# Expert 1's input in sixteen short transfers, and the input of experts 2 and 3 in four

## The chip, the cores and the metric

The kernel runs on one core of a Trainium2 chip. The core has a matrix engine (TensorE, PE in the profile), three engines for elementwise work (VectorE is DVE, ScalarE is ACT, GpSimd is POOL), and SyncE (SP), which here only issues transfers. Transfers between the chip's main memory (DRAM) and the on-chip memory of 128 partitions are carried by 16 DMA engines, which all queues share: a transfer is issued by SyncE, ScalarE or GpSimd and is cut into packets, and the packets are spread over DMA engines. The metric is the device time of one execution in microseconds (us); lower is better.

## The reference

Eight experts, each a two-layer network with its own weights and biases, on 256 rows of 512 numbers:

```python
n_experts, capacity, hidden, expert_hidden = 8, 256, 512, 2048
h = np.matmul(x, w1) + b1[:, np.newaxis, :]
h = np.maximum(h, 0)
return (np.matmul(h, w2) + b2[:, np.newaxis, :]).astype(np.float32)
```

All inputs and the output are float32 in DRAM. Each expert's w1 and w2 are 4 MB each in DRAM.

## The kernel before, in words

Weights are converted to fp16 by the transfer itself, which only GpSimd's queue does here, so each w1 and each w2 is a transfer of 2 MB as written on the chip (128 partitions of 16,384 bytes). w1 and w2 have a pool of three buffers each. Two experts in the list HALVED (6 and 7) load their w2 in two halves, so that their second product can begin on the first.

x reaches the chip in two ways. x of experts 0 and 1 (`nXF32 = 2`, lines 187 to 190) is loaded as float32 by SyncE, 128 rows of 4,096 bytes each (row p of the tile holds rows 2p and 2p + 1 of x); VectorE then casts it to fp16 (line 201). x of experts 2 and 3 is one transfer of GpSimd's queue that converts to fp16 on the way, and x of experts 4 to 7 another (`load_x`, lines 72 to 80; `X_LOADS` gives the first expert and their number). In these, a tile row holds rows of one expert only, and the tile's 128 partitions are shared by the experts. VectorE transposes each x in 32 x 32 blocks (`transposes`, lines 95 to 112) into xT, a pool of two buffers, with the next expert's transposes placed in the middle of an expert's first product (line 135).

`first_product` (lines 114 to 136) makes, for each of sixteen column blocks j, four matmuls into one PSUM tile, which ScalarE then turns into hT with bias and relu (line 128). The bias is read from b1T, which VectorE makes by four transposes of `b1_rows` (line 208). `second_product` (lines 166 to 185) runs three experts later (`LAG = 3`): one small matmul puts b2 into PSUM (line 171), and 2 x 16 matmuls add hT times w2 (line 178). `store` (lines 142 to 164) copies the two PSUM tiles to an output tile, one half by VectorE and one by ScalarE. Experts 0 to 3 and 4 to 5 share an output tile each, which GpSimd's queue writes out at the end (`flush`, lines 138 to 140). Expert 6 is stored in three transfers (`PARTS`, line 40): rows 0 to 24 by SyncE, 25 to 120 by ScalarE, 121 to 127 by SyncE. Expert 7 is one transfer of SyncE.

The order of the work is partly written out and partly chosen by the scheduler of the Tile framework. GpSimd's transfers and all matmuls are kept in program order (`ordered`): w1 of expert 0, the biases b2 and b1, and then what the list `ring` (lines 215 to 225) gives for each step of the main loop: x where `X_LOADS` names the step, w1 of the next experts, w2 of earlier ones. VectorE's order is the scheduler's. In the program before it is: cast x0, sixteen transposes of x0, cast x1, seven transposes of x1, four of the bias, nine of x1, and then the other experts'. The framework gives the transfers of SyncE and ScalarE together eight completion semaphores, and those of GpSimd eight others, in turn; a transfer that takes a semaphore again waits for the one that had it before.

Of the kernel before, what the change touches and what calls it, by code (L numbers as in the profile page):

```python
# [10 lines left out]
def kernel(  # L11
# [9 lines left out]
    nc = tc.nc  # L21
# [4 lines left out]
    P = 128  # L26
    nTB = T // P
# [11 lines left out]

    PARTS = {E - 2: ((0, 25, False), (25, 121, True), (121, 128, False))}  # L40
    nXF32 = 2
    X_LOADS = {2: 2, 4: 4}

    def ordered(ins):
        return tc.keep_in_program_order(ins)
# [26 lines left out]
    def load_x(first, n):  # L72

        R = n * T // P
        t = x_pool.tile([P, R, H], fp16, tag=f"x{first}", name=f"x{first}")
        ordered(nc.gpsimd.dma_start(  # L76
            out=t, in_=x[first : first + n].rearrange("e (p r) h -> (e p) r h", r=R)
        ))
        for i in range(n):
            x16[first + i] = (t, i * (P // n), R)  # L80

    def load_w1(e):
        w1_sb[e] = w1_pool.tile([P, nKC, M], fp16, tag="w1", name="w1sb")
        ordered(nc.gpsimd.dma_start(  # L84
            out=w1_sb[e], in_=w1[e].rearrange("(p kc) m -> p kc m", kc=nKC)
        ))
# [100 lines left out]
    x32 = []  # L187
    for e in range(nXF32):
        x32.append(out_pool.tile([P, nTB, H], fp32, tag="out", name="x32"))
        nc.sync.dma_start(out=x32[e], in_=x[e].rearrange("(p tb) h -> p tb h", tb=nTB))  # L190
    load_w1(0)
    ordered(nc.gpsimd.dma_start(  # L192
        out=b2_sb,
        in_=b2.rearrange("e h -> (e h)").rearrange("(o f) -> o f", o=1),
# [4 lines left out]
    for e in range(nXF32):  # L199
        t = x_pool.tile([P, nTB, H], fp16, tag=f"x{e}", name=f"x{e}")  # L200
# [6 lines left out]
    for b in range(nB):  # L207
        nc.vector.transpose(  # L208
            out=b1T[b * B : (b + 1) * B, nB - 1 - b : nB - 1 - b + nJ * B],
            in_=b1_rows.rearrange("r (i j) -> r j i", j=nJ),  # L210
# [5 lines left out]
    for s in range(1, E + LAG - 1):  # L216
        if s < E:
            if s in X_LOADS:
                ring.append((s - 2, load_x, (s, X_LOADS[s])))
            ring.append((s - 2, load_w1, (s,)))  # L220
        if s >= LAG:
            ring.append((s - 2, load_w2, (s - LAG,)))
# [43 lines left out]
```

## Time and profile before

| | us |
|---|---|
| median of 2 runs (181.54 to 181.85) | 181.69 |
| span of the profiled execution, from the first to the last instruction | 179.8 |
| TensorE matmul busy | 129.0 (72%) |
| VectorE busy | 87.8 (49%) |
| ScalarE busy | 70.2 (39%) |
| GpSimd busy | 13.4 (7%) |

The profile is of one execution; no whole time of that execution is shown beside its span, so the span stands against the median of the runs. Main memory was read 71.39 MB and written 4.19 MB, 420 GB/s over the span. The chain that ended last is put down by 55% to DMA and by 32% to TensorE. Times in rows are from the span's start. A row of a timeline has start, length, engine, line, operation, tiles and count, and in brackets the idle time before it and what ended it; "q" behind an engine's name marks its own sequencer, where transfers are issued. A row of DMA issues has tiles, issuer, count, KB of one and the median from issue to landing.

### The profile page before, as it was taken

To read this page: it belongs to the slowest core of one execution; us is meant where nothing else is said; L and a number is where in the kernel's file an instruction comes from. 1 tells how busy PE (TensorE), PEld (TensorE's weight loads), DVE (VectorE), ACT (ScalarE), POOL (GpSimd) and SP (SyncE) were. 2 spreads that over 40 slices of the span, in tenths; PEclk is the share of its full clock that TensorE was granted. 3 is DMA by queue.
4 is the path that set the end of the run, shared out by engine and by line. 5 is a ranking of instruction groups with operands and counts; after the bars stand their busy time and mean duration, and the time that the engine had idled before them with its cause. 6 is when DMAs were issued, how large, how long until landed. Compare 5 with 4: busy or idle time off the path is not lost.

```text
span 179.8 us, 1957 instructions
## 1 busy us (share of the span) xinstructions
PE 129.0 (72%) x784; PEld 86.2 (48%) x784; DVE 87.8 (49%) x125; ACT 70.2 (39%) x151; POOL 13.4 (7%) x28
## 2 busy tenths in 40 slices
PE   0005199959995930999869597969788887999740
PEld 0004089948993410794369244943387433343310
DVE  1999933985000199999999998000600020301010
ACT  0000569947993050482189005940298020111010
POOL 7000003020201010001000001000100020020000
PEclk9999999987999995599999799996999999999995
DMA  5999999999999999999999999999999999999995
GB/s 215 252 230 195 233 208 201 233 228 200 215 231 193 219 230 222 197 226 230 208 204 230 219 200 226 230 211 200 230 219 201 226 211 208 217 211 221 324 456 215
DMA packets 3828, 40.56 MB, mean 226 GB/s; under 512 B 460, under 2 KB 476, under 8 KB 1132
## 3 DMA queue, kind: packets, MB, share of 16 engines
q0 software_dynamic: 3232, 38.35, 96.5%
q1 hardware_dynamic: 476, 1.70, 2.4%
q10 hardware_dynamic: 112, 0.39, 0.5%
q8 instruction: 6, 0.10, 0.2%
q14 instruction: 2, 0.02, 0.0%
HBM read 71.39 MB, written 4.19 MB: 420 GB/s over the span
## 4 chain that ended last, share of the span: by engine, by line
DMA 55%; PE 32%; ACT 3%; another core or an unknown queue 3%; POOL 2%; issue 1%; POOLq 0%; ACTq 0%
DMA w1sb<-in_w_dram 43%; PE po L178 16%; PE ph L121 15%; DMA w2sb<-in_w_dram 12%; ACT out L157 3%; PE po L171 1%; POOL w1sb L84 1%; ACT hT L128 1%; POOL w2sb L93 0%; POOL x L76 0%; POOL b_sb L192 0%; POOL b_rows L196 0%; POOLq L250 0%; ACTq L128 0%
## 5 line engine op out<-in xcount | busy, mean ns | idle before, releaser
L121 PE MATMUL ph<-xT,w1sb 128*128 128x256 f16 x512 | 64.9, 293 | 34.1 <-DMA w1sb<-in_w_dram 21.5
L121 PEld LDWEIGHTS <-w1sb 128*128 128x128 f16 x512 | 59.8, 147 | 40.1 <-DMA w1sb<-in_w_dram 31.8
L178 PE MATMUL po<-w2sb,hT 128*128 128x512 f16 x256 | 60.0, 394 | 9.8 <-DMA w2sb<-in_w_dram 9.8
L112 DVE STREAM_TRANSPOSE xT<-x 32x256 f16<-32x256 f16 (+1 forms) x64 | 53.0, 888 | 26.0 <-DMA x<-in_x_dram 19.2
L128 ACT ACTIVATE hT<-ph,b1T 128x256 f16<-128x256 f32 x128 | 56.2, 474 | 14.4 <-PE ph L121 14.2
L178 PEld LDWEIGHTS <-hT 128*128 128x128 f16 x256 | 25.5, 101 | 44.1 <-issue 17.8
L156 DVE COPY out<-po 32x512 f32<-32x512 f32 (+2 forms) x22 | 15.1, 688 | 53.7 <-PE po L178 53.5
L157 ACT COPY out<-po 32x512 f32<-32x512 f32 (+2 forms) x22 | 12.7, 579 | 68.8 <-PE po L178 68.6
L109 DVE STREAM_TRANSPOSE xT<-x 32x256 f16<-32x256 f16 x32 | 14.0, 436 | 0.5
L93 POOL DMA_DIRECT2D w2sb<-in_w_dram x10 | 5.3, 534 | 71.6 <-PE po L178 71.6
L84 POOL DMA_DIRECT2D w1sb<-in_w_dram x8 | 4.8, 601 | 64.1 <-PE ph L121 63.3
L128 ACT ACT_TABLE_LOAD x1 | 1.3, 1283 | 20.1 <-DVE b1T L208 20.1
L171 PE MATMUL po<-b_sb,ones 1*128 1x512 f16 x16 | 4.8, 379 | 0.0
L208 DVE STREAM_TRANSPOSE b1T<-b_rows 32x512 f32<-32x512 f32 x4 | 4.1, 1031 | 0.1
L201 DVE CAST x<-x 128x1024 f16<-128x1024 f32 x2 | 1.4, 694 | 3.1 <-DMA x<-in_x_dram 3.1
L171 PEld LDWEIGHTS <-ones 1*128 1x128 f16 x16 | 0.9, 92 | 2.1 <-issue 2.1
L140 POOL DMA_DIRECT2D out_dram<-out x2 | 1.1, 538 | 9.8 <-ACT out L157 9.8
L76 POOL DMA_DIRECT2D x<-in_x_dram x2 | 1.1, 552 | 0.0
L197 DVE MEMSET ones<- 1x128 f16 x1 | 0.2, 165 | 0.8 <-PEq L250 0.8
L196 POOL DMA_DIRECT2D b_rows<-in_b_dram x1 | 0.5, 515 | 0.0
L192 POOL DMA_DIRECT2D b_sb<-in_b_dram x1 | 0.5, 513 | 0.0
L250 POOL MEMSET const-float32-0.0<- 128x1 f32 x1 | 0.1, 99 | 0.2 <-issue 0.2
(3 smaller groups left out, 0.3 us busy)
## 6 DMA issues: line engine op xcount, KB each, us to landing
w1sb<-in_w_dram POOLq DMA_DIRECT2D x8, 2048.0 KB, 34.8
w2sb<-in_w_dram POOLq DMA_DIRECT2D x6, 2048.0 KB, 47.2
w2sb<-in_w_dram POOLq DMA_DIRECT2D x4, 1024.0 KB, 23.2
out_dram<-out POOLq DMA_DIRECT2D x1, 2048.0 KB, 19.0
x<-in_x_dram SPq DMA_DIRECT2D x2, 512.0 KB, 3.7
x<-in_x_dram POOLq DMA_DIRECT2D x1, 1024.0 KB, 31.2
out_dram<-out POOLq DMA_DIRECT2D x1, 1024.0 KB, 14.9
x<-in_x_dram POOLq DMA_DIRECT2D x1, 512.0 KB, 24.0
```

The lines of the kernel that those rows point to most:

```text
L84: ordered(nc.gpsimd.dma_start(out=w1_sb[e], in_=w1[e].rearrange("(p kc) m -> p kc m", kc=nKC)))
L93: ordered(nc.gpsimd.dma_start(out=w2_sb[e][:, lo : lo + half], in_=src[:, lo : lo + half]))
L109: nc.vector.transpose(out=out[:, :, g, :, 0, :], in_=block[:, :, :, 0, :])
L112: nc.vector.transpose(out=out[:, tb, g], in_=block[:, tb])
L121: ordered(nc.tensor.matmul(out=ph, lhsT=w1_sb[e][:, kc, :].rearrange("p (q j) -> p q j", j=nJ)[:, :, j], rhs=xT[e][:, kc, :], start=(kc == 0),
L128: nc.scalar.activation(out=hT[e][:, j, :].rearrange("p (tb k i) -> p tb k i", tb=nTB, k=split), in_=ph.rearrange("p (tb i k) -> p tb k i", ...
L156: nc.vector.tensor_copy(out=out_sb[at : at + rows, k * nTB, :], in_=po[0][part])
L157: nc.scalar.copy(out=out_sb[at : at + rows, k * nTB + 1, :], in_=po[1][part])
L171: ordered(nc.tensor.matmul(out=t, lhsT=ones1, rhs=b2_sb[0:1, e * H : (e + 1) * H], start=True, stop=False,))
L178: ordered(nc.tensor.matmul(out=po[tb], lhsT=hT[e][:, j, tb * P : (tb + 1) * P], rhs=w2_sb[e][:, j, :], start=False, stop=(j == nJ - 1),))
L201: nc.vector.tensor_copy(out=t, in_=x32[e])
L208: nc.vector.transpose(out=b1T[b * B : (b + 1) * B, nB - 1 - b : nB - 1 - b + nJ * B], in_=b1_rows.rearrange("r (i j) -> r j i", j=nJ),)
```

## The change

The load of x1 is cut into sixteen transfers of 15, 14, 13, ..., 2, 1 and 8 rows, issued by SyncE and ScalarE in turn; together they are the same 128 rows. The load of x of experts 2 and 3 is cut into four transfers of 112, 7, 6 and 3 rows, all by GpSimd, in the place of the one before. The load of x of experts 4 to 7 stays whole.

```diff
+    RUNS = ((15, False), (14, True), (13, False), (12, True), (11, False), (10, True), (9, False),
+            (8, True), (7, False), (6, True), (5, False), (4, True), (3, False), (2, True),
+            (1, False), (8, True))
+    X_PARTS = (112, 7, 6, 3)
...
-        ordered(nc.gpsimd.dma_start(
-            out=t, in_=x[first : first + n].rearrange("e (p r) h -> (e p) r h", r=R)
-        ))
+        src = x[first : first + n].rearrange("e (p r) h -> (e p) r h", r=R)
+        at = 0
+        for rows in X_PARTS if first == 2 else (P,):
+            ordered(nc.gpsimd.dma_start(out=t[at : at + rows], in_=src[at : at + rows]))
+            at += rows
+        assert at == P
...
-        nc.sync.dma_start(out=x32[e], in_=x[e].rearrange("(p tb) h -> p tb h", tb=nTB))
+        src = x[e].rearrange("(p tb) h -> p tb h", tb=nTB)
+        at = 0
+        for rows, scalar in RUNS if e == 1 else ((P, False),):
+            (nc.scalar if scalar else nc.sync).dma_start(
+                out=x32[e][at : at + rows], in_=src[at : at + rows])
+            at += rows
+        assert at == P
```

In the program that the scheduler makes of it, VectorE's four bias transposes (line 208 before) now stand ahead of the cast of x1 and its sixteen transposes. TensorE's, ScalarE's and GpSimd's other work keeps its order.

## Prediction, written before the result

> **What bounds the kernel now.** I read the page's slices of the span first, then its DMA queues and issues, then the chain that ended last, and then two tables by stretch.
>
> ```profile
> span 179.8 us, 1957 instructions
> DMA  5999999999999999999999999999999999999995
> q0 software_dynamic: 3232, 38.35, 96.5%
> q1 hardware_dynamic: 476, 1.70, 2.4%
> q10 hardware_dynamic: 112, 0.39, 0.5%
> ...
> x<-in_x_dram SPq DMA_DIRECT2D x2, 512.0 KB, 3.7
> x<-in_x_dram POOLq DMA_DIRECT2D x1, 1024.0 KB, 31.2
> ...
> x<-in_x_dram POOLq DMA_DIRECT2D x1, 512.0 KB, 24.0
> out_dram<-out SPq DMA_DIRECT2D x1, 512.0 KB, 5.3
> out_dram<-out ACTq DMA_DIRECT2D x1, 384.0 KB, 8.1
> out_dram<-out SPq DMA_DIRECT2D x1, 100.0 KB
> b_rows<-in_b_dram POOLq DMA_DIRECT2D x1, 64.0 KB, 13.2
> out_dram<-out SPq DMA_DIRECT2D x1, 28.0 KB
> ```
>
> The reader sees sixteen DMA engines that are busy in every slice but the first and the last. q0 is GpSimd's queue, q1 SyncE's, q10 ScalarE's. No compute engine is the bound; the bound is the work in each DMA engine's own line, and the kernel ends when the last of the sixteen has emptied it.
>
> ```profile
> 4.00 34.59 DMA w1sb<-in_w_dram
> ...
> 147.74 21.57 DMA w2sb<-in_w_dram
> ...
> 169.36 3.63 PE po L178 x16
> ```
>
> That is the chain of waits: start, length, what. At the end the last half of w2 lands at 147.74 + 21.57 = 169.3, sixteen matmuls follow, then the copies and SyncE's last store. By stretch (from:to, length, granted clock, DMA share, GB/s written; a packet counts where it starts, so a share can pass 1):
>
> ```profile
> 1.70:2.20 0.50, 1.00 0.42 74
> 2.20:2.70 0.50, 1.00 0.92 369
> 2.70:3.70 1.00, 1.00 1.02 410
> 3.70:4.20 0.50, 1.00 1.03 418
> 4.20:4.70 0.50, 1.00 1.63 516
> ...
> 48.00:100.00 52.00, 39.22 (x261) 28.39 (x260) 37.08 (x34) 25.85 (x57) 2.99 (x6) 0.90 1.02 217
> ...
> 176.80:177.20 0.40, 0.00 (x0) 0.00 (x0) 0.00 (x0) 0.00 (x0) 0.00 (x0) 0.50 0.86 348
> 177.20:177.60 0.40, 0.00 (x0) 0.00 (x0) 0.00 (x0) 0.00 (x0) 0.00 (x0) 0.50 0.78 317
> 177.60:178.00 0.40, 0.00 (x0) 0.00 (x0) 0.00 (x0) 0.00 (x0) 0.00 (x0) 0.50 0.75 307
> 178.00:178.20 0.20, 0.00 (x0) 0.00 (x0) 0.00 (x0) 0.00 (x0) 0.00 (x0) 0.50 0.27 103
> 178.20:178.40 0.20, 0.00 (x0) 0.00 (x0) 0.00 (x0) 0.00 (x0) 0.00 (x0) 0.50 0.10 41
> 178.40:178.60 0.20, 0.00 (x0) 0.00 (x0) 0.00 (x0) 0.00 (x0) 0.00 (x0) 0.50 0.00 0
> ```
>
> Three things stand here. x of experts 0 and 1 fills the engines from 1.7 to about 4.7, when the long packets of GpSimd's queue first start (share 1.63). From then on there is no gap. At the end the engines do not stop together: a share of 0.78 to 0.75 says that about four stop before 177.6, twelve go on to about 178.0, and the last packet starts before 178.4. So the kernel is within half a microsecond of an even load, and only the longest line counts.
>
> **The change, part by part.** The profiled span is 179.8; the median of the two runs shown is 181.69, so 1.9 lies outside the span, and I add every microsecond of the longest line to 181.69.
>
> *Where the rows go.* Before, each x is 128 rows over 16 engines, eight each. The count of q1's packets tells how a smaller transfer is dealt: three transfers of 128 rows with sixteen end markers each are 432; 476 leaves 44, which is 25 rows with 5 markers and 7 rows with 7. So 25 rows went on 5 engines and 7 rows on 7 (q10: 96 rows and 16 markers are its 112). A transfer of up to 15 rows thus gives one row to each of as many engines. If each starts with engine 0, engine e gets one row from every run longer than e: engine 0 sixteen, engine 4 twelve, engine 7 nine, engine 8 seven, engine 14 one, engine 15 none. The trace does not name engines; that the first ones are taken is my choice, because both odd stores have the same form.
> The Trainium skill, in "DMA: Bandwidth & Descriptors", section "Why a DMA increments its semaphore by 16 and not by 1", says that SyncE and ScalarE transfers take the lowest-numbered engines, as many as the row count's largest divisor up to 16; by that rule the packet counts agree.
>
> *Price of a row.* From 2.70 to 3.70 the two x loads wrote 410 GB/s: 410,000 bytes in 1 us over 16 engines, at 4,096 bytes 6.26 rows for one engine, 0.160 us a row. Against eight rows, x1 gives engine 0 8 × 0.160 = +1.28, engine 1 +1.12, engine 2 +0.96, engine 3 +0.80, engine 4 +0.64, engine 8 -0.16, engine 15 -1.28.
>
> *What the high engines gain.* Little at the start: GpSimd's packets begin near 4.6, and an engine with few rows of x1 is through with x0 near 3.1 and waits for them. The low engines' extra rows are served between GpSimd's packets later, so theirs is real work in a line that never rests.
>
> *GpSimd's four parts.* 112 rows are seven for each engine. A row of 4,096 bytes written costs 16 × 4,096 / 217,000 = 0.302 us in the middle stretch. For the 7, 6 and 3 there is no row in this trace. One end: each part starts with engine 0, then engines 0 to 2 have ten rows, +0.60, 3 to 5 have nine, +0.30, and 7 to 15 seven, -0.30. Other end: the parts follow one another round the engines (7 + 6 + 3 = 16), nothing changes, 0. Nearest are the two odd stores, which I take as starting on the same engine: +0.60 on engine 0.
> By another rule of the same section of the Trainium skill GpSimd's queue deals a part of less than 16 shares from a cursor that goes round; by that the term would be 0 and the sum 182.6. The section names an exception too, some copies that put one share on each of the first engines, which would be the +0.60. No run shows either yet.
>
> *Which engines are last now.* Expert 6's store (25, 96 and 7 rows) puts 5 + 6 + 1 = 12 rows on engines 0 to 4, seven on 5 and 6 and six on the rest. So 0 to 4 carry 6 × 0.160 = 0.96 more than 7 to 15, which is the width of the end seen above (177.2 to 178.2). I take them as part of the group that ends near 178.0, 0.4 before the last packet's start.
>
> *The sum.* Engine 0: -0.4 + 1.28 + 0.60 = +1.48. The added end markers are nine or ten short packets on an engine; at nothing. 181.69 + 1.48 = 183.2. With 0 for GpSimd's parts it is 182.6; if engine 0 or 1 is the last one already, 181.69 + 1.88 = 183.6, and the other way, if engine 0 ends near 177.6, 182.8.
>
> *Issues and waits.*
>
> ```profile
> 0.74 0.87 SPq L190 DMA_DIRECT2D x<-in_x_dram  x2
> 164.81 9.18 SPq L164 DMA_DIRECT2D out_dram<-out  x3
> ...
> 2.41 0.52 POOL L196 DMA_DIRECT2D b_rows<-in_b_dram  x1
> ...
> 3.48 0.56 POOL L76 DMA_DIRECT2D x<-in_x_dram  x1
> 4.00 0.91 POOL L84 DMA_DIRECT2D w1sb<-in_w_dram  x1
> 29.93 0.53 POOL L84 DMA_DIRECT2D w1sb<-in_w_dram  x1 [25.03 <-PE ph L121]
> ...
> 20.14 1.28 ACT L128 ACT_TABLE_LOAD   x1 [20.14 <-DVE b1T L208]
> ...
> 12.03 0.69 DVE L201 CAST x<-x 128x1024 f16<-128x1024 f32 x1
> 12.76 3.13 DVE L109 STREAM_TRANSPOSE xT<-x 32x256 f16<-32x256 f16 x7
> 15.90 4.17 DVE L208 STREAM_TRANSPOSE b1T<-b_rows 32x512 f32<-32x512 f32 x4
> 20.09 4.04 DVE L109 STREAM_TRANSPOSE xT<-x 32x256 f16<-32x256 f16 x9
> ```
>
> SyncE issues nine loads for two, ScalarE eight for none, at 0.87 / 2 = 0.44 each: 3.5 us a queue. There are eight completion semaphores for the two queues, so from 9 rows on each waits for the transfer eight before it; SyncE's 9 rows wait for x0 (0.74 + 3.7 = 4.4), its 1 row waits for the 9 rows. These late rows stand behind GpSimd's packets, which at four times the row and 217 for 410 GB/s take 0.160 × 4 × 410 / 217 = 1.2 us each; a row and its marker take two turns. I estimate x1 complete at 13 to 16, for 5 before. ScalarE is bound only at 20.14; SyncE at 164.8. Cover: the built program puts the four b1T transposes ahead of x1's cast. They wait for the biases (2.41 + 13.2 = 15.6, later by up to 1.3 on engine 0), so b1T ends near 21 instead of 20.07, and ScalarE's first activation moves by about 1; x1 is cast at 21 and its sixteen transposes (3.13 + 4.04 = 7.2) end at 29, for 24.1. Expert 1's product starts after expert 0's, about 29.9 (the w1 buffer that POOL waits for), so 0 to 1.5 us go, and come back at the next wait: expert 2's w1 lands only at 4.00 + 34.59 = 38.59. Without that cover, x1 later than 23 would cost TensorE time, though not yet DMA time.
> GpSimd issues three more, 3 × 0.56, and through the same eight semaphores its third w1 now waits for the first to land (about 16 for 4.00). The queue still holds x2 until 3.48 + 24.0 = 27.5: nothing. The fourth w1 at about 31 stands ahead of 38.59: nothing.
> The Trainium skill, same page, section "Rules for kernel authors", speaks against it: under 64 KB a transfer is mostly overhead, coalesce. With that page's 2.0 us a transfer an estimate is nine in a row, 18 us for x1, still before 21: by that the sum stays.
>
> **The rivals.** First: every added transfer halts the engines. For it: between 1.70 and 2.70 the shares 0.42 and 0.92 say that a start lost 0.29 + 0.04 = 0.33 us on all engines. Fifteen in the loaded queue would be 5.0; 181.69 + 5.0 = 186.7. Against it: the first start meets an empty queue, and x1's start right behind (2.70 to 4.20, shares 1.02 and 1.03) lost nothing. It decides from 3.6 / 15 = 0.24 us each. Chance 0.07.
> Second: the high engines are the late ones and the low ones have room, so the change evens the end. For it: four engines do stop early, and the store of expert 6 already favours the high ones. Gain at most to the mean end, about 0.5: 181.2. Against it: engine 0 would have to be among the early four by 1.9. Chance 0.08.
> Third: the change does not tilt anything, since transfers are dealt in turn: 15 + 14 + ... + 1 + 8 is 128, 7 + 6 + 3 is 16, both even if dealt round. Time 181.7. Chance 0.11; against it are the 25 and 7 rows if they overlap.
>
> **How the numbers follow.** Forecast (the low engines end last) 0.74, its own range 182.4 to 183.9. A measurement of this kernel tells about 2% (3.6 us) from no change: the forecast, the second and the third lie within it. Slower by over 2% is the first rival and a little for x1 coming very late, 0.08; faster by over 2% would need less work in the lines than the same bytes, 0.01; same 0.91. The range takes the third rival in: 181.6 to 184.2.
>
> **What the profile of the changed kernel would show.** q1 460 packets (144 + 64 + 64 + 144 + 30 + 14) and q10 240 (64 + 64 + 112): the dealing is right. DMA share near 0.5 between 3 and 4.6, on the way to GpSimd's start: the high engines idle there. At the end a share that falls slowly from about 177 to 179.9 instead of from 176.8 to 178.4: the tilt. Last w2 within 0.7 of 169.3. x1's cast at 20 to 22; if it is later than 25, the cover was misjudged. A share under 1 between 5 and 16 speaks for the first rival, an end before 178.4 for the second, an unchanged one for the third.

## The result, and the profile after

The changed kernel takes 184.16 us, median of 2 runs (184.10 to 184.23), for 181.69 before: a ratio of 1.013, 95% interval 1.0099 to 1.0162, +2.47 us. The profiled span went from 179.8 to 182.3. It is slower by less than 2%, as forecast, and inside the range of 181.6 to 184.2, but only by 0.04 us; it is above the forecast's own range (182.4 to 183.9). The direction was right, and the size, +1.48, was too small by 1.0 us.

The page of the changed kernel, its slices, its queues and GpSimd's loads of x2 and the biases (tiles, issuer, count, KB, median from issue to landing):

```profile
span 182.3 us, 1983 instructions
...
DMA  7999999999999999999999999999999999999992
...
q0 software_dynamic: 3312, 38.35, 95.1%
q1 hardware_dynamic: 460, 1.44, 2.2%
q10 hardware_dynamic: 240, 0.66, 1.2%
...
x<-in_x_dram POOLq DMA_DIRECT2D x1, 448.0 KB, 25.4
...
b_rows<-in_b_dram POOLq DMA_DIRECT2D x1, 64.0 KB, 15.4
...
x<-in_x_dram POOLq DMA_DIRECT2D x1, 28.0 KB, 25.4
...
x<-in_x_dram POOLq DMA_DIRECT2D x1, 24.0 KB, 25.2
...
x<-in_x_dram POOLq DMA_DIRECT2D x1, 12.0 KB, 25.0
```

The same bytes (38.35 MB on q0), no gap in the middle, but a last slice of 2 tenths where it was 5: the tail is longer and thinner. q1 has 460 packets and q10 240, both exactly as worked out, so short transfers are dealt one row to each of as many engines as they have rows.

The chain of waits of the changed kernel (start, length, what), its start and its end:

```profile
2.43 15.36 DMA b_rows<-in_b_dram
...
149.54 21.60 DMA w2sb<-in_w_dram
171.18 3.63 PE po L185 x16
```

The last half of w2 lands at 171.14, 1.8 later than before; the sixteen matmuls behind it take the same 3.63. The end by stretch (from:to, length, granted clock, DMA share, GB/s written):

```profile
176.80:177.60 0.80, 0.58 1.00 415
177.60:178.40 0.80, 0.50 0.44 184
178.40:179.20 0.80, 0.50 0.39 164
179.20:180.00 0.80, 0.50 0.35 143
180.00:180.80 0.80, 0.50 0.11 46
180.80:181.60 0.80, 0.50 0.00 0
```

And the same stretches of the kernel before:

```profile
176.80:177.60 0.80, 0.50 0.82 333
177.60:178.40 0.80, 0.50 0.47 189
178.40:179.20 0.80, 0.50 0.00 0
```

Before, all sixteen engines have started their last packet by 178.4. After, a share of 0.44, then 0.39 and 0.35 says that about six engines work on for 2 us while ten have nothing left, if an engine that has work does not pause (the trace does not name the engines). That fits the tilt that the prediction described, and it is longer than its 179.9.

The timeline of the changed kernel for the steps of the start (start, length, engine, line, operation, tiles, count, idle time and what ended it):

```profile
3.50 2.07 POOL L83 DMA_DIRECT2D x<-in_x_dram  x4
...
17.02 0.57 POOL L91 DMA_DIRECT2D w1sb<-in_w_dram  x1 [11.45 <-DMA w1sb<-in_w_dram]
17.81 4.17 DVE L221 STREAM_TRANSPOSE b1T<-b_rows 32x512 f32<-32x512 f32 x4 [4.51 <-DMA b_rows<-in_b_dram]
22.01 0.69 DVE L214 CAST x<-x 128x1024 f16<-128x1024 f32 x1
22.06 1.28 ACT L135 ACT_TABLE_LOAD   x1 [22.06 <-DVE b1T L221]
...
31.41 0.54 POOL L91 DMA_DIRECT2D w1sb<-in_w_dram  x1 [13.82 <-PE ph L128]
```

x1's cast at 22.01 waits for nothing: it stands right behind the bias transposes, so x1 had landed under their cover. The fourth w1 is issued at 31.41, 1.5 later than before, and the engines show no gap there.

### The profile page after: what moved, and what is told of

Same layout as the page of the kernel before. It is cut to its first block, busy times and chain, and to the rows that moved or that the text cites. A ratio compares the mean times of both kernels' runs of the same rounds, so it can differ in the third digit from the quotient of the medians.

```text
span 182.3 us, 1983 instructions
## 1 busy us (share of the span) xinstructions
PE 127.5 (70%) x784; PEld 86.5 (47%) x784; DVE 87.5 (48%) x125; ACT 70.7 (39%) x151; POOL 14.6 (8%) x31
## 3 DMA queue, kind: packets, MB, share of 16 engines
q0 software_dynamic: 3312, 38.35, 95.1%
## 4 chain that ended last, share of the span: by engine, by line
DMA 64%; PE 20%; DVE 7%; issue 2%; POOL 1%; ACT 1%; another core or an unknown queue 0%; DVEq 0%; ACTq 0%; POOLq 0%
DMA w1sb<-in_w_dram 27%; DMA x<-in_x_dram 17%; PE ph L128 14%; DMA w2sb<-in_w_dram 12%; DMA b_rows<-in_b_dram 8%; PE po L185 6%; DVE xT L119 5%; DVE b1T L221 2%; ACT L135 1%; POOL w1sb L91 1%; POOL w2sb L100 0%; ACT out L164 0%; PE po L178 0%; POOL b_sb L205 0%; ACT hT L135 0%
## 5 line engine op out<-in xcount | busy, mean ns | idle before, releaser
L128 PE MATMUL ph<-xT,w1sb 128*128 128x256 f16 x512 | 66.7, 298 | 41.0 <-DMA w1sb<-in_w_dram 28.9
L128 PEld LDWEIGHTS <-w1sb 128*128 128x128 f16 x512 | 60.9, 148 | 47.7 <-DMA w1sb<-in_w_dram 39.1
L185 PE MATMUL po<-w2sb,hT 128*128 128x512 f16 x256 | 56.7, 379 | 6.3 <-DMA w2sb<-in_w_dram 6.3
L185 PEld LDWEIGHTS <-hT 128*128 128x128 f16 x256 | 24.7, 98 | 38.1 <-issue 9.8
L83 POOL DMA_DIRECT2D x<-in_x_dram x5 | 2.6, 550 | 0.0
```

What stands on the lines that cost most here:

```text
L83: ordered(nc.gpsimd.dma_start(out=t[at : at + rows], in_=src[at : at + rows]))
L128: ordered(nc.tensor.matmul(out=ph, lhsT=w1_sb[e][:, kc, :].rearrange("p (q j) -> p q j", j=nJ)[:, :, j], rhs=xT[e][:, kc, :], start=(kc == 0),
L185: ordered(nc.tensor.matmul(out=po[tb], lhsT=hT[e][:, j, tb * P : (tb + 1) * P], rhs=w2_sb[e][:, j, :], start=False, stop=(j == nJ - 1),))
```

## The experiments

My theory after the result is that of the lines: each DMA engine works through a line of its own, the kernel ends with the longest, and the short transfers of all three queues put their rows on the same first engines. The rivals: the count (what costs is the number of transfers, wherever their rows go) and the late start (x1 and the biases come later, and the whole chain behind them). All ratios are against the kernel before on the same chip, where it took 181.55 to 181.70. The scheduler puts VectorE's order together anew for each kernel, and that turned out to matter.

**The two halves of the change, each alone.** runs_only keeps x1's sixteen transfers; parts_only keeps GpSimd's four parts.

```diff
 # runs_only
-    X_PARTS = (112, 7, 6, 3)
+    X_PARTS = (P,)
 # parts_only
-    RUNS = ((15, False), (14, True), ... (8, True))
+    RUNS = ((P, False),)
```

Expected of runs_only:

> Only x1's sixteen transfers; x of experts 2 and 3 whole. Theory of the lines (the longest line of a DMA engine sets the end, and the short transfers all start on the same first engine): engine 0 gets eight rows more, in the loaded queue with a marker each, so +1.3 to +1.8 on 181.7, 183.0 to 183.5. Theory of the count (each added transfer costs all engines the same, 2.47 / 18 = 0.14 each): 15 x 0.14 = +2.1, 183.8. Theory of the late start (bias transposes and first activation come about 2 later and that is carried to the end): the whole +2.5, 184.2.

Measured: 183.42 us, ratio 1.0102 (1.0085 to 1.0119), +1.87.

Expected of parts_only:

> Only the four parts 112, 7, 6 and 3 of GpSimd; x1 whole. Theory of the lines: engines 0 to 2 get two rows of 0.30 more, +0.6 at most, less by what they now end before the last one; 181.9 to 182.3. If the parts were dealt round the engines: 181.7. Theory of the count: 3 x 0.14 = +0.4, 182.1. Theory of the late start: 181.7, since VectorE's order is the one before.

Measured: 182.20, ratio 1.0033 (1.0021 to 1.0046), +0.65. Together 2.52, for 2.47 of the whole change: the two add up, as they must if they load the same line (a cost by the count would add up too). The end of runs_only and then of parts_only by stretch (columns as above):

```profile
177.60:178.40 0.80, 0.50 0.47 195
178.40:179.20 0.80, 0.50 0.39 159
179.20:180.00 0.80, 0.50 0.20 82
180.00:180.80 0.80, 0.50 0.00 0
```

```profile
177.60:178.40 0.80, 0.50 0.48 195
178.40:179.20 0.80, 0.50 0.20 82
179.20:180.00 0.80, 0.50 0.00 0
```

The tail of parts_only is about three engines wide (0.20) and ends by 179.2, as three engines with ten rows of x2 each would make it; that of runs_only is wider (0.39, six engines) and one stretch longer.

**As many transfers of x1, but without a tilt.** even16 cuts x1 into sixteen transfers of 16 rows by half a row each, so every engine gets one packet of every transfer; SyncE and ScalarE still take turns, and x2 is whole.

```diff
+        if e == 1:
+            for i in range(16):
+                p, c = 16 * (i // 2), i % 2
+                (nc.scalar if c else nc.sync).dma_start(
+                    out=x32[e][p : p + 16, c, :], in_=src[p : p + 16, c, :])
+            continue
```

Expected:

> x1 in sixteen transfers of 16 rows by half a row, by SyncE and ScalarE in turn: as many transfers as in the change, and each engine gets sixteen half rows, so no line is longer. Theory of the lines: 181.7 to 182.1 (only the markers are added). Theory of the count: +2.1, 183.8. Theory of the late start: x1 is here cast ahead of the bias transposes and lands late, so ScalarE starts even later than with the change, and the time is 184 or more.

Measured: 184.38 (183.03 to 185.2), ratio 1.0146 (1.0112 to 1.0179), +2.83. By the lines it should have cost nearly nothing, and the count gave 183.8. The late start gave 184 or more for this kernel, because x1 is cast ahead of the bias transposes in it. The trace of even16 shows how that goes; first its timeline, then its DMA share by stretch:

```profile
19.55 0.69 DVE L216 CAST x<-x 128x1024 f16<-128x1024 f32 x1 [6.94 <-DMA x<-in_x_dram]
...
27.18 1.28 ACT L135 ACT_TABLE_LOAD   x1 [27.18 <-DVE b1T L223]
...
37.91 0.53 POOL L91 DMA_DIRECT2D w1sb<-in_w_dram  x1 [33.35 <-PE ph L128]
```

```profile
30.00:36.00 6.00, 1.00 1.02 218
36.00:38.00 2.00, 1.00 0.05 8
```

Here the scheduler put x1's cast ahead of the bias transposes. VectorE waited for x1 until 19.55, the biases came behind its transposes, ScalarE began at 27.18 instead of 22.06, and GpSimd's fourth w1 was issued at 37.91, when its queue had run empty: 2 us at a share of 0.05. So in this kernel a late start does cost time, and the run doesn't separate the tilt from it, as it was made to.

**x1 in two transfers, tilted.** two_tilted loads x1 in 119 and 9 rows by SyncE: 119 rows are 17 each on 7 engines, so engines 0 to 6 carry 18 rows of x1 each, ten more than before, with one transfer added.

```diff
+    RUNS = ((119, False), (9, False))
+    X_PARTS = (P,)
```

Expected:

> x1 in two transfers of SyncE, of 119 and 9 rows: by the rule that the row count's largest divisor up to 16 is the number of engines, 7 engines get 17 rows each and then 9 engines one. Theory of the lines: engines 0 to 6 get ten rows more at 0.16, 183.1 to 183.4, though only one transfer is added. Theory of the count: +0.14, 181.8. Theory of the late start: x1 lands by 8 at the latest, ahead of its cast at 12, so 181.7.

Measured: 184.72 (184.05 to 185.88), ratio 1.0175 (1.0146 to 1.0205), +3.17, more than any of the three figures. It has the same trouble as even16 (x1's cast at 18.42, ScalarE from 26.50, fourth w1 at 35.78), so both were made again with VectorE's order held as in the changed kernel:

```diff
-        nc.vector.tensor_copy(out=t, in_=x32[e])
+        ordered(nc.vector.tensor_copy(out=t, in_=x32[e]))
...
-        nc.vector.transpose(
+                ordered(nc.vector.transpose(
```

with the four bias transposes moved ahead of x1's cast in the program. Expected of even16_bias_first:

> As even16 (sixteen transfers of x1 that load all sixteen engines alike), but with the bias transposes kept ahead of x1's cast, so that expert 0's activations, and with them GpSimd's fourth w1, come early enough. Theory of the lines: the loss of even16 (the queue ran empty near 38) goes, and what is left is the markers and turns of sixteen short transfers on every engine: 181.7 to 182.3. Theory of the count: still +2.1, 183.7.

Measured: 182.17 (182.10 to 182.29), ratio 1.0030 (1.0020 to 1.0039), +0.55. Expected of two_tilted_bias_first:

> As two_tilted (119 and 9 rows, so 18 rows on engines 0 to 6), bias transposes kept ahead of x1's cast. Theory of the lines: ten rows more on seven engines, at 0.16 to 0.23 a row +1.6 to +2.3 on 181.6: 183.2 to 183.9, with one added transfer. Theory of the count: 181.7.

Measured: 184.15 (183.88 to 184.34), ratio 1.0133 (1.0114 to 1.0152), +2.53. The end of even16_bias_first by stretch, and the two rows of its timeline that differ from even16:

```profile
177.60:178.40 0.80, 1.00 0.70 287
178.40:179.20 0.80, 0.73 0.13 51
```

```profile
21.36 1.28 ACT L135 ACT_TABLE_LOAD   x1 [21.36 <-DVE b1T L221]
...
31.94 0.53 POOL L91 DMA_DIRECT2D w1sb<-in_w_dram  x1 [27.37 <-PE ph L128]
```

This pair decides. Sixteen transfers that load all engines alike cost 0.55; two that load seven engines with ten rows more cost 2.53. The count falls. The late start as the main cost of the change falls too: even16_bias_first has ScalarE start and the fourth w1 go out as late as the changed kernel, within 0.7 us, and costs a fifth of it. In two_tilted_bias_first the fourth w1 goes out another 1.2 us later (33.17); two_tilted_act_cast, below, takes that difference away. What the 0.55 is made of stays open: end markers, the late start that is left, or the dip that is left at 36 to 37 us (a share of 0.39 there). The size of two_tilted_bias_first missed high (183.2 to 183.9 were expected): 0.25 us for each of ten rows, for 0.16 to 0.23.

**The tilt of eight engines at once.** runs_of_8 loads x1 in sixteen transfers of 8 rows, so engines 0 to 7 carry all of it, sixteen rows each.

```diff
+    RUNS = tuple((8, i % 2 == 1) for i in range(16))
+    X_PARTS = (P,)
```

Expected:

> x1 in sixteen transfers of 8 rows by SyncE and ScalarE in turn, GpSimd's x whole. Engines 0 to 7 get sixteen rows each, 8 to 15 none: 64 rows moved for 36 in the runs of 15 to 1, but the longest line is the same sixteen. Theory of the lines (only the longest counts): as runs_only, 183.2 to 183.7. A cost by the rows moved: 181.55 + 1.87 x 64 / 36 = 184.9. Theory of the count: as runs_only.

Measured: 184.35 (183.86 to 185.3), ratio 1.0148 (1.0125 to 1.0172), +2.73. Neither figure holds. Engine 0 has as many rows as in runs_only and the kernel takes 0.9 more, so the longest line's row count alone does not give the time when eight lines are long together. Its trace shows one thing that runs_only lacks; first its last half of w2 (start, length), then its end by stretch:

```profile
149.58 22.86 DMA w2sb<-in_w_dram
```

```profile
176.00:176.80 0.80, 1.00 0.62 266
176.80:177.60 0.80, 1.00 0.48 205
177.60:178.40 0.80, 1.00 1.14 466
```

That half lands at 172.44, 1.9 us later than in runs_only (170.57). About half of the engines run dry before the last store, which has to wait for w2's matmuls and copies, and the share rises again when the store's packets come. So here the chain of work behind the last w2 has a part in the end as well; how large a part is not shown.

**GpSimd's parts, twice as heavy.** x4_parts cuts x of experts 4 to 7 instead, whose rows are twice as long (1,024 KB for 512), and leaves x1 and x2 whole.

```diff
+    RUNS = ((P, False),)
...
-        for rows in X_PARTS if first == 2 else (P,):
+        for rows in X_PARTS if first == 4 else (P,):
```

Expected:

> The four parts 112, 7, 6 and 3 on the load of x of experts 4 to 7, whose row is twice as long, in place of that of 2 and 3; x1 and the other x whole. Theory of the lines: two rows of 0.60 more on engines 0 to 2, twice the +0.65 of parts_only: 182.7 to 182.9. Theory of the count: the same three transfers, as parts_only, 182.2.

Measured: 182.78 (182.53 to 182.98), ratio 1.0058 (1.0042 to 1.0074), +1.16. Twice the bytes in the same number of transfers, 1.8 times the cost (1.16 / 0.65): it is the bytes of the parts that cost and not their number. That is what three parts make that start on the same engine; dealt round, they would add nothing.

**Expert 6's store in one piece.** The odd store (25, 96 and 7 rows) puts twelve rows on engines 0 to 4 where an even one puts eight. after_plain_store takes it out of the changed kernel, before_plain_store out of the kernel before.

```diff
-    PARTS = {E - 2: ((0, 25, False), (25, 121, True), (121, 128, False))}
+    PARTS = {}
```

Expected of after_plain_store:

> The changed kernel with expert 6 stored in one transfer of 128 rows: engines 0 to 4 have eight rows of it for twelve, engines 7 to 15 eight for six. Theory of the lines (engines 0 and next are last with the change): 4 x 0.16 = -0.64 on 184.16, 183.5. If the high engines were last: +0.3, 184.5. Theory of the count: two transfers less, -0.3, 183.9.

Measured: 183.50, ratio 1.0093 (1.0071 to 1.0115): 0.66 less than the changed kernel, for 4 rows × 0.160 = 0.64, though the two intervals still touch (the changed kernel's begins at 1.0099). Expected of before_plain_store:

> The kernel before with expert 6 stored in one transfer. Theory of the lines: engines 0 to 4 end 0.64 earlier, but some of 7 to 15 end about where they do and get 2 x 0.16 = 0.32 more: 181.5 to 182.0, so the same edit helps the changed kernel and does not help this one. Theory of the count: -0.3, 181.3.

Measured: 182.03, ratio 1.0017 (1.0000 to 1.0035), +0.33. The same edit helps the changed kernel and, if anything, costs the kernel before, where the high engines then get two rows more (2 × 0.160 = 0.32) and must already have stood near the end too. This agrees with the lines in both signs; the engines themselves are in no row, so the last step is argued.

**Is it the end markers?** If two_tilted_bias_first cost more than its rows because of something that comes with each transfer, four transfers should show it. four_tilted_bias_first loads x1 in 55, 35, 25 and 13 rows by SyncE: 5 + 5 + 5 + 1 = 16 rows on engines 0 to 4, as runs_only puts on engine 0 with sixteen transfers. The edit is against two_tilted_bias_first.

```diff
-    RUNS = ((119, False), (9, False))
+    RUNS = ((55, False), (35, False), (25, False), (13, False))
```

Expected:

> x1 in four transfers of SyncE, of 55, 35, 25 and 13 rows (eleven, seven, five and thirteen engines by the largest divisor), bias transposes first: engines 0 to 4 get sixteen rows, the same as engine 0 with the runs of 15 to 1, in four transfers for sixteen. If the 0.6 by which runs_only went over 8 x 0.16 = 1.28 came from the markers and turns of sixteen short transfers: 181.6 + 1.3 = 182.9. If an added row costs 0.23 to 0.25 however it is cut (as in two_tilted_bias_first): 183.4 to 183.6.

Measured: 183.67 (183.64 to 183.98), ratio 1.0118 (1.0100 to 1.0136), +2.07: 0.26 for each of eight added rows, with four transfers; runs_only has 0.23 with sixteen. So the number of transfers does not raise the cost of a row here. The two kernels differ in a second way, though: five engines have sixteen rows of x1 here and only one in runs_only, and runs_of_8 shows that the number of long lines counts too. A small cost of markers could hide behind that.

**x0's cast on ScalarE.** In two_tilted_bias_first GpSimd's first packets came late. two_tilted_act_cast moves the cast of x0 from VectorE to ScalarE, to see whether that start has a part in the time.

```diff
+        if e == 0:
+            nc.scalar.copy(out=t, in_=x32[e])
+        else:
+            ordered(nc.vector.tensor_copy(out=t, in_=x32[e]))
```

Expected:

> As two_tilted_bias_first, with x0's cast on ScalarE in place of VectorE. In the runs so far GpSimd's first packets come between 3.7 and 4.2 where VectorE casts x0 at 4.8 or later, and after 4.2 where it casts near 4.0. If VectorE's cast holds back GpSimd's first transfer, the packets now start between 3.7 and 4.2, for 4.7 to 5.2; if not, as there. The time: the longest lines do not wait for that start, so 183.8 to 184.2 by the theory of the lines; if the start sets the end, 183.3 or less.

Measured: 183.98 (183.88 to 184.24), ratio 1.0132 (1.0117 to 1.0147). The start came earlier (last section) and the time stayed within 0.2 us: the long line does not care when it begins by half a microsecond. This kernel also closes the rival of the late start. Its fourth w1:

```profile
31.97 0.54 POOL L89 DMA_DIRECT2D w1sb<-in_w_dram  x1 [27.41 <-PE ph L126]
```

That is the moment of even16_bias_first (31.94), and ScalarE's first activation is as late in both, within 0.1 us. The tilted kernel costs 2.38, the even one 0.55. None of the twelve kernels beats the one before.

## Why the prediction was right or wrong

**The dealing was right.** 460 and 240 packets, and the 476 and 496 that q1 has in two_tilted_bias_first and four_tilted_bias_first, are what the dealing gives. That all of them start on the same engine is in no row, but the times fit it: runs_only, two_tilted_bias_first and four_tilted_bias_first cost more the more rows this puts on engine 0, and even16_bias_first, dealt evenly, costs little.

**GpSimd's parts were right.** 2 rows × 0.302 = 0.60 was taken, +0.65 measured alone, and +1.16 for 2 × 0.604 = 1.21 with rows of twice the length. The four parts of the changed kernel land within about 1.2 us of one another (issued half a microsecond apart, 25.4, 25.4, 25.2 and 25.0 under way), which does not tell how they were dealt; the times do. For such a queue the Trainium skill, "DMA: Bandwidth & Descriptors", section "Why a DMA increments its semaphore by 16 and not by 1", has a rule with a cursor that goes round, by which the parts would be free, and an exception that gives some direct copies one share on each engine from the first on. These runs agree with the exception and not with the cursor (182.20 where it gives 181.55).

**The offset failed.** "I take them as part of the group that ends near 178.0, 0.4 before the last packet's start": the -0.4 of the sum is not there. With it parts_only would have cost 0.2 and x4_parts 0.8; they cost 0.65 and 1.16. So engine 0 must have stood at the end line already, and before_plain_store says that the high engines stood near it too. I had read it from a share that falls from 0.75 to 0.27 and 0.10 around 178.0, which are four engines and then one or two; which ones these are the trace doesn't say, and the sum's own alternative ("if engine 0 or 1 is the last one already", 183.6) was the one to take.

**The term of x1 was too small.** "0.160 us a row" came from a stretch in which both x loads had the engines to themselves. Measured, an added row costs 1.87 / 8 = 0.23 (runs_only), 2.07 / 8 = 0.26 (four_tilted_bias_first), 2.53 / 10 = 0.25 (two_tilted_bias_first) and 2.73 / 8 = 0.34 (runs_of_8). With 0.23 and no offset the sum is 8 × 0.23 + 0.60 = 2.44, for 2.47 measured, which is no test of its own, since 0.23 comes from one half of the change. The sum with 0.160 and no offset gave 1.88; so of the 1.0 us that was missing, 0.4 is the offset and 0.6 lies in the eight rows of x1. Whether those 0.6 are the price of a row is open. All four kernels also start late (fourth w1 between 31.3 and 33.8, for 29.93 before), as even16_bias_first does (31.94), which costs 0.55 without a tilt. Taken off, runs_only leaves 1.32 / 8 = 0.165 a row, close to the prediction's price, but four_tilted_bias_first and two_tilted_bias_first still leave 0.19 and 0.20. In the store at the end, where the engines write 333 to 415 GB/s for 217 in the middle, 0.160 fits (after_plain_store, 0.66 / 4, within its noise).

**That it fell inside the range was luck.** The highest figure that the working reaches is 183.6; nothing in it gives the range's upper end of 184.2, and the two errors of 0.4 and 0.6 went the same way.

**Last w2 "within 0.7 of 169.3" failed**: 171.14. It lands in the same long line, so it had to move with the sum: in two_tilted_bias_first and two_tilted_act_cast it is issued 1.5 apart (151.32 and 149.83) and lands within 0.1 (171.69 and 171.57), so the queue ahead of it sets when it lands, and not its issue. parts_only moves it by 0.1 (147.84 + 21.59 = 169.43), runs_only by 1.3 (149.00 + 21.57 = 170.57), the whole change by 1.8. In parts_only the end moves by 0.6 with w2 nearly still, so the tail is not merely the compute chain behind w2.

**The cover held.** x1's cast at 22.01 was given as 20 to 22, the third and fourth w1 as about 16 and 31 (17.02 and 31.41). The biases landed at 2.43 + 15.36 = 17.8, a microsecond later than allowed for, and ScalarE's first activation moved by 1.9 instead of 1. No gap in the engines shows for it, and even16_bias_first, nearly as late, puts its cost at 0.55 at most. even16 shows what it costs without that cover: the fourth w1 6.5 us later than this, 2 us of idle DMA, 2.2 us more than with the order held (184.38 for 182.17). The prediction named the cover but said that losing it "would cost TensorE time, though not yet DMA time"; at 37.91 it does cost DMA time.

**The rivals.** The first (every added transfer halts the engines) is refuted by even16_bias_first: 0.55 for fifteen transfers, at most 0.04 each, where it needs 0.24. The second (the low engines have room) by parts_only, the third (nothing tilts) by both halves.

**The start was misread in one point.** A share "near 0.5 between 3 and 4.6" was expected of high engines waiting for GpSimd's packets. The changed kernel by stretch:

```profile
2.70:3.70 1.00, 1.00 0.75 303
3.70:4.20 0.50, 1.00 1.65 467
```

The dip is there (0.75), but those packets begin before 4.2, not near 4.6.

## What to carry to other kernels

In a kernel like this one, whose sixteen DMA engines never rest, the end moves with the longest lines though the bytes stay the same: before cutting a transfer into odd sizes, count the rows that each part puts on the first engine, and price a row in the loaded stretch. If a transfer must be cut, give every part sixteen rows; fifteen more such transfers cost 0.55 us here, while parts that put eight more rows on one engine cost 1.9. And after any edit near a scheduler, compare its order before comparing times: one cast that moved ahead of four transposes was worth 2.2 us.

## What the runs showed of the hardware

GpSimd's first packets can be held up while VectorE casts; two kernels suggest it and a third does not fit. The two kernels with x1 in two parts, first with x0's cast on VectorE, its timeline and its stretches:

```profile
3.97 0.69 DVE L212 CAST x<-x 128x1024 f16<-128x1024 f32 x1 [2.99 <-DMA x<-in_x_dram]
```

```profile
3.70:4.20 0.50, 1.00 0.76 221
4.20:4.70 0.50, 1.00 0.47 180
4.70:5.20 0.50, 1.00 1.50 303
```

and then two_tilted_act_cast, with the cast on ScalarE:

```profile
3.98 1.04 ACT L213 CAST x<-x 128x1024 f16<-128x1024 f32 x1 [1.97 <-DMA x<-in_x_dram]
```

```profile
3.70:4.20 0.50, 1.00 1.05 270
4.20:4.70 0.50, 1.00 2.07 410
```

While VectorE casts, the share is 0.47 and the burst of new packets comes after it, at 4.7; with the same cast on ScalarE the burst (2.07) comes half a microsecond earlier. In the changed kernel x0's cast is at 5.39, and the burst comes ahead of it. The Trainium skill, "SBUF — State Buffer", section "SBUF: two separate sides", says that GpSimd cannot write descriptors while VectorE runs an fp32 copy in its two-port mode; this pair agrees. It does not settle the matter: in four_tilted_bias_first, too, VectorE casts x0 early, and the burst comes during the cast:

```profile
4.10 0.69 DVE L212 CAST x<-x 128x1024 f16<-128x1024 f32 x1 [3.11 <-DMA x<-in_x_dram]
```

```profile
4.20:4.70 0.50, 1.00 1.89 344
```

Why it is not held up there stays open. In the pair it cost nothing: 184.15 and 183.98.

q0 has 80 packets more than before for three more transfers (in parts_only all 80 are under 512 bytes), where sixteen end markers each would be 48. Where the other 32 come from stays open.
